# Clears off GpSimd, a later place for the decay's powers, the mixer's state recurrence on VectorE, and the last early modulation moved into the first feed-forward

## The chip, the cores and the metric

One core of a Trainium2 chip runs the whole program. The metric is the time of one execution on the device in microseconds (us); lower is better. TensorE (PE in the profile) multiplies matrices, VectorE (DVE), ScalarE (ACT) and GpSimd (POOL) work element by element, and SyncE (SP) issues nearly all transfers from the chip's memory.

## The reference

`first_block` followed by `second_block`, on 256 tokens of 1024 features in float32. Only the first block is touched by the change:

```python
mod = silu(cond) @ w_mod + b_mod                       # 9 vectors of 1024: shift, scale, gate three times
(sh1, sc1, g1, sh2, sc2, g2, sh3, sc3, g3) = split(mod, 9)
h = modulate(rms_norm(x, ffn1_norm), sh1, sc1)
x = x + 0.5 * g1 * swiglu(h, ffn1_w_gate, ffn1_w_up, ffn1_w_down)
h = modulate(rms_norm(x, mix_norm), sh2, sc2)
b_gate, c_gate, v, u = split(h @ w_in, 4)
y_conv = short_conv_mixer(b_gate, c_gate, v, conv_w)   # b_gate * conv3(c_gate * v)
y_ssm = s5_mixer(u, ...)                               # linear recurrence with complex decay, gelu, gated unit
x = x + g2 * (concat(rms_norm(y_conv), rms_norm(y_ssm)) @ w_out)
h = modulate(rms_norm(x, ffn2_norm), sh3, sc3)         # sc3 is modulation 7
x = x + 0.5 * g3 * swiglu(h, ffn2_...)
```

## The kernel before

**Precision and weights.** Every weight matrix comes in tiles of 128x2048 float32 (1 MB) through three buffers called `stage`. A tile is split into two parts: ScalarE rounds it to `wh` (line 185), VectorE takes the rest `wl = stage - wh` (line 187). A product is then three TensorE products. `Stream.schedule()` fixes the order of all tiles; `Stream.prep` loads and splits them in that order as far as four slots for split weights allow, and a transfer is issued when the tile three places ahead of it in the order has been used up.

**Modulations.** A tile of `w_mod` (a "chunk"; four chunks make one modulation) isn't split: VectorE multiplies it by the condition and adds it into `macc` with two instructions of 128x1024 (lines 853 and 855). `macc` has two buffers, and a modulation's buffer is free once TensorE has summed it over the partitions (`mod_reduce`, lines 871 and 876). Modulations 0 and 1 come first, 2 to 6 within the first feed-forward (`ffn1`), 7 within the mixer.

**The first feed-forward.** `turn` multiplies the first weights while the tokens are brought over: `evac(0)` and `evac(1)` modulate the two halves of the tokens into `hT`. Then come steps 1 to 10. A step has two products `up` (gate and up), the hidden tile (`hidf`, line 477), one product `acc` with an earlier `down` tile, and a side piece. All instructions of an engine run in the order in which the code issues them.

**The state-space set-up.** `Ssm` clears its buffers (lines 592 to 595), then computes the decay on GpSimd in `prepare`, its powers in `powers`, and from a TensorE transpose on (`s_end`, in steps 2 to 4) the `readout` and the `tables`; steps 7 to 9 make the lag kernel (`s_lag`). `powers` has one VectorE instruction, the reciprocal of line 680, between GpSimd ones.

**The mixer.** Projections `proj(ch)` alternate with the convolution (`conv_a`, `conv_v`, `conv_b`) and the recurrence (`turning(h)`, two halves, lines 1139 to 1152), whose 14 instructions are shared by VectorE (`vt`) and GpSimd (`gt`). `outputs(h)` multiplies the states, `gelu(h)` moves them on.

Of the kernel before, what the change touches and what calls it, by code (L numbers as in the profile page):

```python
# [31 lines left out]

MODS_FFN1 = (2, 3, 4, 5, 6)
MODS_MIXER = (7,)
MODS_FFN2 = (8,)
# [20 lines left out]
def schedule():  # L56
# [4 lines left out]
    def w(name, i=0):  # L61
        it.append((name, i))
# [42 lines left out]
    swap(2)  # L105
    md = [4 * g + c for g in MODS_MIXER for c in range(4)]
    for c in (6, 7, 2, 4, 0, 3, 5, 1):
        w("w_in", c)
        if c in (0, 3, 5, 1):
            w("w_mod", md.pop(0))  # L110
    w("w_out", 0)
# [96 lines left out]
class Net:  # L208
# [219 lines left out]
    def turn(self, tail, evac, chunks, use):  # L428
# [5 lines left out]
        if tail is None:  # L434
            evac(0)
            evac(1)
        else:
            for part in tail.parts[0]:
                part()
            tail.post(0)  # L440
            early = len(tail.parts[1]) - tail.late
            for part in tail.parts[1][:early]:
                part()
            S.prep(S.n_take + 1)
            evac(0)
            for part in tail.parts[1][early:]:
                part()
            S.prep(S.n_take + 2)
            tail.post(1)
            if self.after_tail is not None:  # L450
                self.after_tail()
                self.after_tail = None
            S.prep(S.n_take + n_c)
# [124 lines left out]
class Ssm:  # L578


    def __init__(self, N, p):
        self.N, self.p = N, p
        t = N.t2
        self.out = [t([16, 160], "s_out%d" % c) for c in range(2)]
        self.end = [t([16, 128], "s_end%d" % c) for c in range(2)]
        self.lag = t([16, 128], "s_lag")
        p0 = t([2, 16, 32], "s_tab2")
        self.p0 = [p0[:, c] for c in range(2)]
        self.small = t([24, 16], "s_small")
        g = N.nc.gpsimd  # L590
        self.first()
        g.memset(p0, 0.0)
        for c in range(2):
            g.memset(self.out[c], 0.0)
        g.memset(self.lag, 0.0)

# [121 lines left out]
    def step(self, s):  # L718

        N = self.N  # L720
        nc = N.nc
        if 2 <= s <= 4:
            for b in ((0, 1), (2, 3, 4), (5, 6, 7))[s - 2]:
                c, q0 = divmod(4 * b, 16)
# [4 lines left out]
                nc.scalar.copy(out=self.end[c][:, q0:q0 + 4, :], in_=pv)  # L729
            if s == 4:  # L730
                self.readout()
                self.tables()
# [64 lines left out]
def build(N):  # L797
# [117 lines left out]
    mod_reduce(1, lambda: N.bank_a("mod"))  # L915
    ssm.powers()
    xns = {}
# [31 lines left out]
    def side1(s):  # L949
# [4 lines left out]
    tail_places("ffn1_w_down", 10, 0)  # L954
    tail = N.ffn(None, lambda i: N.evac_mod(pts[i], i, modf[:, 1, :], modf[:, 0, :], N.hT),
                 ("ffn1_w_gate", "ffn1_w_up"), "ffn1_w_down", 11, True, post_ffn1, side1, 1)
    mods_ready()


    tail = mixer(N, tail, evac_mod(1), ssm, dict(  # L960
        convw=sv["conv_w"], glub=sv["glu_b"], onorm=sv["out_norms"], ones=ones, xns=xns, mods=mods_ready))

# [86 lines left out]
def mixer(N, tail, evac, ssm, c):  # L1049
    nc, t, take = N.nc, N.t, N.take  # L1050
    ones, onorm = c["ones"], c["onorm"]
    x = N.x
    vt, gt, act = nc.vector.tensor_tensor, nc.gpsimd.tensor_tensor, nc.scalar.activation
    us, cts = [], []
# [29 lines left out]

    def proj(ch):
        ps = N.bank_u("proj")
        N.feat(take("w_in", ch), N.hT, v3(ps, 2))
        N.S.free()
        return ps
# [17 lines left out]

    def conv_b(h):
        ks = slice(2 * h, 2 * h + 2)
        vt(out=flat(yc[:, ks, :]), in0=proj(h), in1=flat(conv_in[h]), op=MUL)  # L1110
        act(out=yq[:, ks, :], in_=yc[:, ks, :], func=AF.Square)
# [7 lines left out]
    conv_a(0, ps)  # L1119
    conv_v(0, vps)  # L1120

# [11 lines left out]
    def turning(h, m):  # L1133
# [6 lines left out]
        vt(out=m[1], in0=wi, in1=sin, op=MUL)  # L1140
        gt(out=m[0], in0=m[0], in1=m[1], op=ADD)
        vt(out=m[2], in0=wi, in1=cos, op=MUL)
        vt(out=m[3], in0=wr, in1=sin, op=MUL)
        gt(out=m[2], in0=m[2], in1=m[3], op=SUB)
        nc.vector.tensor_tensor_scan(out=m[1], data0=rho, data1=m[0], initial=0.0, op0=MUL, op1=ADD)
        vt(out=sr, in0=m[1], in1=cos, op=MUL)
        gt(out=si, in0=m[1], in1=sin, op=MUL)
        nc.vector.tensor_tensor_scan(out=m[3], data0=rho, data1=m[2], initial=0.0, op0=MUL, op1=ADD)
        vt(out=m[0], in0=m[3], in1=sin, op=MUL)
        gt(out=m[2], in0=m[3], in1=cos, op=MUL)  # L1150
        vt(out=sr, in0=sr, in1=m[0], op=SUB)
        gt(out=si, in0=si, in1=m[2], op=ADD)

# [25 lines left out]

    turning(0, [t([512], "hm", bufs=2), t([512], "hm", bufs=2)] + pair(t([1024], "macc", bufs=2)))  # L1180
    turning(1, [t([512], "hidh1"), t([512], "hidl1")] + pair(t([1024], "macc", bufs=2)))
    conv_b(0)
    conv_a(1, proj(3))
    outputs(0)
    gelu(0)
    conv_v(1, proj(5))
    conv_b(1)
    outputs(1)

# [11 lines left out]
    for k in range(4):  # L1201
        gain_split(yc, 0, k, hc)
    hy = (t([4, S], "hTh", F32R), t([4, S], "hTl", F32R))
    y[1] = N.t2([2, 4, 64], "s_tab0")
# [18 lines left out]
    conv_part(0, 1)  # L1223
    c["mods"]()
    ps = sums(yq)
# [683 lines left out]
```

## Time and profile before

| | |
|---|---|
| median of three runs | 1220.27 us (1218.33 to 1220.82) |
| the profiled execution | 1219.3 us |
| its span in the profile | 1217.6 us |
| granted TensorE clock, mean | 0.959 |
| busy share: TensorE, VectorE, ScalarE, GpSimd | 93%, 65%, 50%, 19% |

The span is that of one execution under the profiler; 1.7 us of its own time lie outside it. Terms below are made against 1219.3 us, and the median lies 1.0 us above that. A busy TensorE is not one at full rate, so waits are read from rows and not from its share.

### The profile page before, as it was taken

How to read it: one execution, taken by the hardware profiler on the slowest of the kernel's cores; microseconds unless marked ns; L12 is line 12 of the kernel's file. 1: busy time of each engine (PE TensorE's matmuls, PEld its weight loads, DVE VectorE, ACT ScalarE, POOL GpSimd, SP SyncE). 2: the span in 40 equal slices, each digit the busy share in tenths (PEclk: the TensorE clock that was granted, in tenths of full speed). 3: DMA queues.
4: the chain of work that ended last, by engine and by line, in shares of the span. 5: the costliest groups of instructions: out<-in, count | busy, mean ns of one | idle time of the engine just before them, and what ended most of it. 6: DMA issues, size and time to landing. Idle time of an engine off the chain costs nothing.

```text
span 1217.6 us, 18757 instructions
## 1 busy us (share of the span) xinstructions
PE 1135.3 (93%) x7780; PEld 1051.7 (86%) x7780; DVE 793.7 (65%) x934; ACT 613.4 (50%) x941; POOL 236.6 (19%) x304
## 2 busy tenths in 40 slices
PE   1698999989789999999798999999999899999998
PEld 1697999979778999998798889999989897999997
DVE  7698797667968785565466665644468776564541
ACT  3444434455084554354364656655446764664541
POOL 8996399400500000000224100000000000000000
PEclk9698999989789999999897999999999899999999
DMA  8588787535243786565043245755625332385540
GB/s 318 225 327 308 249 322 281 202 139 208 88 155 139 260 324 213 189 242 181 30 144 135 90 141 202 251 178 199 205 107 194 118 118 108 124 291 194 183 143 35
DMA packets 33093, 230.13 MB, mean 189 GB/s; under 512 B 3680, under 2 KB 4064, under 8 KB 5872
## 3 DMA queue, kind: packets, MB, share of 16 engines
q1 hardware_dynamic: 31536, 224.05, 51.2%
q10 hardware_dynamic: 1472, 4.88, 1.1%
q8 instruction: 61, 1.00, 0.3%
q14 instruction: 24, 0.20, 0.0%
HBM read 227.87 MB, written 1.05 MB: 188 GB/s over the span
## 4 chain that ended last, share of the span: by engine, by line
PE 66%; DVE 16%; ACT 8%; POOL 4%; issue 3%; DMA 2%; ACTq 0%; DVEq 0%; POOLq 0%
PE acc L262 26%; PE up L262 25%; PE turn L262 7%; DVE wl L187 7%; ACT wh L185 2%; PE kqv L262 2%; DVE macc L855 1%; POOL s_small L626 1%; PE xnT L349 1%; POOL s_small L629 1%; PE lev L1385 1%; DMA stage<-in_ffn_w_up 1%; PE glu L262 1%; ACT s_lag L748 1%; POOL E L1363 1%
## 5 line engine op out<-in xcount | busy, mean ns | idle before, releaser
L187 DVE TENSOR_TENSOR wl<-stage,wh 128x1024 fp32r<-128x1024 f32 x351 | 425.7, 1261 | 131.3 <-ACT wh L185 131.1
L185 ACT CAST wh<-stage 128x1024 fp32r<-128x1024 f32 x351 | 346.8, 1045 | 126.1 <-PE acc L262 31.4
L262 PE MATMUL up<-hTh,wh 128*128 128x256 f32 x1024 | 289.2, 282 | 1.9 <-ACT s_end L729 1.9
L262 PE MATMUL up<-hTl,wh 128*128 128x256 f32 x1024 | 287.8, 281 | 0.0
L262 PE MATMUL up<-hTh,wl 128*128 128x256 f32 x1024 | 287.8, 281 | 0.0
L262 PEld LDWEIGHTS up<-hTh,wh 128*128 128x128 f32 x1024 | 193.9, 189 | 4.4 <-ACT s_end L729 2.3
L262 PEld LDWEIGHTS up<-hTh,wl 128*128 128x128 f32 x1024 | 196.2, 192 | 0.0
L262 PEld LDWEIGHTS up<-hTl,wh 128*128 128x128 f32 x1024 | 193.6, 189 | 1.5 <-issue 0.2
L262 PE MATMUL acc<-wh,hidh 128*128 128x512 f32 x288 | 115.0, 399 | 4.0 <-ACT wh L185 3.7
L262 PE MATMUL acc<-wl,hidh 128*128 128x512 f32 x288 | 114.0, 396 | 0.8 <-DVE wl L187 0.8
L262 PE MATMUL acc<-wh,hidl 128*128 128x512 f32 x288 | 113.9, 395 | 0.3 <-DVE hidl L296 0.3
L262 PE MATMUL turn<-wh,hTh 128*128 128x256 f32 x320 | 91.4, 286 | 6.2 <-ACT hTh L290 6.2
L262 PE MATMUL turn<-wl,hTh 128*128 128x256 f32 x320 | 90.9, 284 | 2.1 <-DVE wl L187 2.1
L262 PE MATMUL acc<-wh,macc 128*128 128x512 f32 x288 | 92.7, 391 | 0.0
L262 PE MATMUL turn<-wh,hTl 128*128 128x256 f32 x320 | 91.0, 285 | 0.2 <-DVE hTl L291 0.2
L855 DVE SCALAR_TENSOR_TENSOR macc<-stage,cact,macc 128x1024 f32<-128x1024 f32 x63 | 86.1, 1367 | 3.1 <-DMA stage<-in_w_mod 1.4
L262 PEld LDWEIGHTS acc<-wh,hidh 128*128 128x128 f32 x288 | 55.1, 191 | 15.5 <-ACT wh L185 4.1
L262 PEld LDWEIGHTS turn<-wh,hTh 128*128 128x128 f32 x320 | 61.3, 192 | 6.8 <-ACT hTh L290 6.5
L262 PEld LDWEIGHTS acc<-wh,hidl 128*128 128x128 f32 x288 | 54.9, 191 | 13.3 <-DVE hidl L296 1.0
L262 PEld LDWEIGHTS acc<-wl,hidh 128*128 128x128 f32 x288 | 55.0, 191 | 12.1 <-DVE wl L187 1.8
L262 PEld LDWEIGHTS turn<-wl,hTh 128*128 128x128 f32 x320 | 61.2, 191 | 3.1 <-DVE wl L187 2.8
L262 PEld LDWEIGHTS acc<-wh,macc 128*128 128x128 f32 x288 | 54.1, 188 | 11.0
(401 smaller groups left out, 2020.0 us busy)
## 6 DMA issues: line engine op xcount, KB each, us to landing
stage<-in_w SPq DMA_DIRECT2D x64, 1024.0 KB, 4.8
stage<-in_w_mod SPq DMA_DIRECT2D x36, 1024.0 KB, 4.9
stage<-in_ffn_w_gate SPq DMA_DIRECT2D x22, 1024.0 KB, 4.8
stage<-in_ffn_w_up SPq DMA_DIRECT2D x22, 1024.0 KB, 5.0
stage<-in_ffn_w_down SPq DMA_DIRECT2D x22, 1024.0 KB, 5.2
stage<-in_a_in SPq DMA_DIRECT2D x12, 1024.0 KB, 4.9
stage<-in_w_in SPq DMA_DIRECT2D x8, 1024.0 KB, 5.0
stage<-in_w_kv SPq DMA_DIRECT2D x8, 1024.0 KB, 4.9
```

Source lines behind the costliest of these rows:

```text
L185: nc.scalar.copy(out=h[:, b:e], in_=st[:, b:e])
L187: nc.vector.tensor_tensor(out=lo[:, b:e], in0=st[:, b:e], in1=h[:, b:e].bitcast(F32), op=SUB)
L262: self.nc.tensor.matmul(out, lhs(l, k), rhs(r, k), start=first and n == 0, stop=last and n == 3 * n_k - 1)
L349: self.nc.tensor.transpose(out, src, self.ident)
L626: g.tensor_tensor(out=o, in0=x, in1=y, op=op)
L629: g.tensor_scalar(out=o, in0=x, scalar1=s1, scalar2=s2, op0=op0, op1=op1)
L748: nc.scalar.copy(out=self.lag[32 * i:32 * i + 32, 4 * b:4 * b + 4, 32 * i:128], in_=ks[:32, :, 0:128 - 32 * i])
L855: nc.vector.scalar_tensor_tensor(out=acc, in0=wv[:, k, :], scalar=cc, in1=acc, op0=MUL, op1=ADD)
L1363: gt(out=ev[:, :, 1, :], in0=bv[:, :, 1, :], in1=ref, op=SUB)
L1385: nc.tensor.matmul(ps[:, 64 * e:64 * e + 64], ks[:, 128 * e:128 * e + 128], qs[:, 64 * e:64 * e + 64], start=True, stop=True)
```

## The change

Five pieces. (1) The clears of the two `out` buffers go from GpSimd to VectorE, that of `lag` to ScalarE; they are issued first. (2) `powers` is called after the second evacuation, not ahead of the first, and the second weight is split between the two evacuations. (3) The transposes `s_end`, and what follows them on GpSimd, go from steps 2 to 4 to steps 3 to 5. (4) Modulation 7's four chunks go from the mixer into `ffn1`. (5) In the mixer all of `turning` runs on VectorE; its first half stands ahead of the first convolution, its second half behind the projections 0, 3 and 5; `gelu(0)` comes after the convolution's gain, and the last projection's `take` no longer runs ahead.

```diff
-MODS_FFN1 = (2, 3, 4, 5, 6)
-MODS_MIXER = (7,)
+MODS_FFN1 = (2, 3, 4, 5, 6, 7)
...
     for c in (6, 7, 2, 4, 0, 3, 5, 1):
         w("w_in", c)
-        if c in (0, 3, 5, 1):
-            w("w_mod", md.pop(0))
...
             evac(0)
+            S.prep(S.n_take + 2)
             evac(1)
...
-        self.first()
         g.memset(p0, 0.0)
         for c in range(2):
-            g.memset(self.out[c], 0.0)
-        g.memset(self.lag, 0.0)
+            N.nc.vector.memset(self.out[c], 0.0)
+        self.first()
+        N.nc.scalar.activation(out=self.lag, in_=N.ident.unsqueeze(1).to_broadcast([128, 16, 128]), func=AF.Copy, scale=0.0)
...
-        if 2 <= s <= 4:
-            for b in ((0, 1), (2, 3, 4), (5, 6, 7))[s - 2]:
+        if 3 <= s <= 5:
+            for b in ((0, 1), (2, 3, 4), (5, 6, 7))[s - 3]:
...
-            if s == 4:
+            if s == 5:
                 self.readout()
                 self.tables()
...
-    ssm.powers()
...
+    def evac_first(i):
+        N.evac_mod(pts[i], i, modf[:, 1, :], modf[:, 0, :], N.hT)
+        if i:
+            ssm.powers()
...
-    conv_v(0, vps)
...
-        gt(out=m[0], in0=m[0], in1=m[1], op=ADD)
+        vt(out=m[0], in0=m[0], in1=m[1], op=ADD)
...
     turning(0, [t([512], "hm", bufs=2), t([512], "hm", bufs=2)] + pair(t([1024], "macc", bufs=2)))
+    conv_v(0, vps)
+    conv_b(0, proj(0))
+    conv_a(1, proj(3))
+    vps = proj(5)
     turning(1, [t([512], "hidh1"), t([512], "hidl1")] + pair(t([1024], "macc", bufs=2)))
-    conv_b(0)
-    conv_a(1, proj(3))
     outputs(0)
-    gelu(0)
-    conv_v(1, proj(5))
-    conv_b(1)
+    conv_v(1, vps)
+    conv_b(1, proj(1, 0))
     outputs(1)
...
         gain_split(yc, 0, k, hc)
+    gelu(0)
...
-    c["mods"]()
```

Three places on VectorE, in the order in which it runs its instructions. The first is at the two evacuations (`hm`, `hTl`) ahead of the first products; before, the reciprocal stands ahead of both:

```order
L882 SCALAR_TENSOR_TENSOR modf<-modf,pack 128x8
L680 RECIPROCAL s_small<-s_small 128x16
L380 TENSOR_SCALAR hm<-xnT,modf 128x128 x4
L291 TENSOR_TENSOR hTl<-hm,hTh 128x4x128 x2
L380 TENSOR_SCALAR hm<-xnT,modf 128x128 x4
L291 TENSOR_TENSOR hTl<-hm,hTh 128x4x128 x2
L187 TENSOR_TENSOR wl<-stage,wh 128x1024 x2
```

And in the changed kernel, where the reciprocal stands behind both and the second weight's split between them:

```order
L879 SCALAR_TENSOR_TENSOR modf<-modf,pack 128x8
L376 TENSOR_SCALAR hm<-xnT,modf 128x128 x4
L287 TENSOR_TENSOR hTl<-hm,hTh 128x4x128 x2
L183 TENSOR_TENSOR wl<-stage,wh 128x1024 x2
L376 TENSOR_SCALAR hm<-xnT,modf 128x128 x4
L287 TENSOR_TENSOR hTl<-hm,hTh 128x4x128 x2
L677 RECIPROCAL s_small<-s_small 128x16
```

What moved: the reciprocal went six rows down, and `wl` two rows up.

The second place is the mixer from the copies of `u4` (`gate<-macc`) on, before. Three more chunks of modulation 7 (`macc<-stage`) and the convolution `conv_v(0)` stand ahead of the first half of the recurrence (`hm<-ssm_w`):

```order
L1079 COPY gate<-macc 32x4x64 x6
L187 TENSOR_TENSOR wl<-stage,wh 128x1024 x2
L855 SCALAR_TENSOR_TENSOR macc<-stage,cact,macc 128x1024 x2
L187 TENSOR_TENSOR wl<-stage,wh 128x1024 x2
L855 SCALAR_TENSOR_TENSOR macc<-stage,cact,macc 128x1024 x2
L1098 TENSOR_TENSOR hidh<-proj,act 128x512
```

And in the changed kernel:

```order
L1079 COPY gate<-macc 32x4x64 x6
L183 TENSOR_TENSOR wl<-stage,wh 128x1024 x4
L1138 TENSOR_TENSOR hm<-ssm_w,s_tab 128x512
L1139 TENSOR_TENSOR hm<-ssm_w,s_tab 128x512
L1140 TENSOR_TENSOR hm<-hm 128x512
L1141 TENSOR_TENSOR macc<-ssm_w,s_tab 128x512
```

What moved: the chunks are gone, the recurrence follows the splits, and its sums (line 1140) are VectorE's.

The third place is step 3 of the first feed-forward, changed kernel, between the hidden tiles (`hidf`) of steps 2 and 3:

```order
L474 TENSOR_TENSOR hidf<-up,act 128x512
L287 TENSOR_TENSOR xn<-hidf,xn 128x512
L183 TENSOR_TENSOR wl<-stage,wh 128x1024 x2
L869 TENSOR_TENSOR gate<-mod,gate 128x512 x2
L183 TENSOR_TENSOR wl<-stage,wh 128x1024 x2
L852 SCALAR_TENSOR_TENSOR macc<-stage,cact,macc 128x1024 x2
L183 TENSOR_TENSOR wl<-stage,wh 128x1024 x2
L850 TENSOR_SCALAR macc<-stage,cact 128x1024
L852 SCALAR_TENSOR_TENSOR macc<-stage,cact,macc 128x1024 x3
```

What moved: the last two rows hold two chunks where the step had one, and so it is in the steps 2 to 5 by VectorE's order.

## Rows read from the trace of the kernel before

**Rows 1.** Busy time by stretch: PE, PEld, DVE, ACT, POOL, granted clock, DMA share, GB/s

```profile
60.00:110.00 50.00, 45.17 (x298) 41.15 (x297) 47.05 (x38) 20.97 (x25) 48.56 (x40) 0.90 0.87 319
110.00:150.00 40.00, 40.00 (x308) 38.05 (x307) 28.20 (x26) 19.54 (x25) 8.94 (x10) 1.00 0.75 268
286.60:352.40 65.80, 54.56 (x423) 54.10 (x422) 57.07 (x66) 24.14 (x40) 18.96 (x18) 0.85 0.45 166
```

**Rows 2.** Timeline to the first products: start, time, engine, line, instruction, [idle before <- releaser]

```profile
5.92 4.41 POOL L594 MEMSET s_out<- 128x2560 f32 x2
6.40 6.22 DVE L853 TENSOR_SCALAR macc<-stage,cact 128x1024 f32<-128x1024 f32 x1 [6.40 <-DMA stage<-in_w_mod]
...
13.67 0.63 ACT L311 ACTIVATE hm<-x 128x512 bf16<-128x512 f32 x1 [8.41 <-DMA x<-in_x]
13.96 12.28 SPq L156 DMA_DIRECT2D stage<-in_w_mod  x5
...
24.60 9.21 DVE L855 SCALAR_TENSOR_TENSOR macc<-stage,cact,macc 128x1024 f32<-128x1024 f32 x7
...
41.45 0.25 DVE L680 RECIPROCAL s_small<-s_small 128x16 f32<-128x16 f32 x1 [3.57 <-POOL s_small L626]
...
43.59 0.58 PE L262 MATMUL turn<-wh,hTh 128*128 128x256 f32 x1 [6.16 <-ACT hTh L290]
```

**Rows 3.** TensorE's wait for a split, 44 to 250 us: total, times, longest

```profile
PE turn L262 <- DVE wl L187: 1.1, 1, 1.1
```

**Rows 4.** VectorE's groups from 60 to 110 us: count | busy, mean ns | idle before

```profile
L187 DVE TENSOR_TENSOR wl<-stage,wh 128x1024 fp32r<-128x1024 f32 x18 | 25.5, 1462 | 1.4 <-ACT wh L185 1.4
L855 DVE SCALAR_TENSOR_TENSOR macc<-stage,cact,macc 128x1024 f32<-128x1024 f32 x11 | 16.7, 1517 | 0.2
```

**Rows 5.** The split's group from 114 to 142 us

```profile
L187 DVE TENSOR_TENSOR wl<-stage,wh 128x1024 fp32r<-128x1024 f32 x8 | 9.4, 1222 | 4.5 <-ACT wh L185 4.5
```

**Rows 6.** VectorE's timeline in the first feed-forward, steps 2 to 7

```profile
98.43 0.68 DVE L477 TENSOR_TENSOR hidf<-up,act 128x512 f32<-128x512 f32 x1
...
124.33 2.36 DVE L187 TENSOR_TENSOR wl<-stage,wh 128x1024 fp32r<-128x1024 f32 x2 [3.40 <-ACT wh L185]
...
189.81 0.68 DVE L477 TENSOR_TENSOR hidf<-up,act 128x512 f32<-128x512 f32 x1
```

**Rows 7.** The chain that ended last, in order of time: start, time, what

```profile
69.97 4.82 DMA stage<-in_ffn_w_up
...
102.19 13.67 PE up L262 x96
...
122.63 10.91 PE up L262 x96
```

**Rows 8.** GpSimd's timeline at the transposes

```profile
142.21 0.40 POOL L768 TENSOR_SCALAR s_out<-s_tab 64x256 f32<-64x256 f32 x1 [19.56 <-PE s_end L349]
```

**Rows 9.** VectorE's groups in the mixer, 286 to 353 us

```profile
L855 DVE SCALAR_TENSOR_TENSOR macc<-stage,cact,macc 128x1024 f32<-128x1024 f32 x7 | 9.0, 1283 | 0.2
L1148 DVE TENSOR_TENSOR_SCAN macc<-s_tab,macc 128x512 f32<-128x512 f32 x2 | 4.6, 2281 | 0.0
...
L1142 DVE TENSOR_TENSOR macc<-ssm_w,s_tab 128x512 f32<-128x512 f32 x2 | 1.4, 686 | 0.0
...
L1145 DVE TENSOR_TENSOR_SCAN hidl<-s_tab,hidh 128x512 f32<-128x512 f32 x1 | 1.2, 1225 | 0.1
...
L853 DVE TENSOR_SCALAR macc<-stage,cact 128x1024 f32<-128x1024 f32 x1 | 0.7, 747 | 0.0
```

**Rows 10.** VectorE's timeline in the mixer

```profile
308.15 0.69 DVE L1139 TENSOR_TENSOR hm<-ssm_w,s_tab 128x512 f32<-128x512 f32 x1
...
328.46 3.42 DVE L187 TENSOR_TENSOR wl<-stage,wh 128x1024 fp32r<-128x1024 f32 x2
...
369.12 1.06 DVE L1247 TENSOR_TENSOR s_end<-xn,s_ttmp 128x256 f32<-128x256 f32 x2
```

More of the change, by code (lines that the diff above doesn't have):

```diff
@@ L105, in schedule @@
     swap(2)
-    md = [4 * g + c for g in MODS_MIXER for c in range(4)]
     for c in (6, 7, 2, 4, 0, 3, 5, 1):
         w("w_in", c)
-        if c in (0, 3, 5, 1):
-            w("w_mod", md.pop(0))
     w("w_out", 0)
@@ L954, in build @@
     tail_places("ffn1_w_down", 10, 0)
-    tail = N.ffn(None, lambda i: N.evac_mod(pts[i], i, modf[:, 1, :], modf[:, 0, :], N.hT),
-                 ("ffn1_w_gate", "ffn1_w_up"), "ffn1_w_down", 11, True, post_ffn1, side1, 1)
+    def evac_first(i):
+        N.evac_mod(pts[i], i, modf[:, 1, :], modf[:, 0, :], N.hT)
+        if i:
+            ssm.powers()
+    tail = N.ffn(None, evac_first, ("ffn1_w_gate", "ffn1_w_up"), "ffn1_w_down", 11, True, post_ffn1, side1, 1)
     mods_ready()
     tail = mixer(N, tail, evac_mod(1), ssm, dict(
-        convw=sv["conv_w"], glub=sv["glu_b"], onorm=sv["out_norms"], ones=ones, xns=xns, mods=mods_ready))
+        convw=sv["conv_w"], glub=sv["glu_b"], onorm=sv["out_norms"], ones=ones, xns=xns))
     def after_mixer():
@@ L1052, in mixer @@
     x = N.x
-    vt, gt, act = nc.vector.tensor_tensor, nc.gpsimd.tensor_tensor, nc.scalar.activation
+    vt, act = nc.vector.tensor_tensor, nc.scalar.activation
     us, cts = [], []
@@ L1083, in mixer, with proj @@
     cw = c["convw"]
-    def proj(ch):
+    def proj(ch, ahead=10 ** 9):
         ps = N.bank_u("proj")
-        N.feat(take("w_in", ch), N.hT, v3(ps, 2))
+        N.feat(take("w_in", ch, ahead), N.hT, v3(ps, 2))
         N.S.free()
@@ L1106, in conv_v, with conv_b @@
         conv_in[h] = o
-    def conv_b(h):
+    def conv_b(h, ps):
         ks = slice(2 * h, 2 * h + 2)
-        vt(out=flat(yc[:, ks, :]), in0=proj(h), in1=flat(conv_in[h]), op=MUL)
+        vt(out=flat(yc[:, ks, :]), in0=ps, in1=flat(conv_in[h]), op=MUL)
         act(out=yq[:, ks, :], in_=yc[:, ks, :], func=AF.Square)
@@ L1140, in turning @@
         vt(out=m[1], in0=wi, in1=sin, op=MUL)
-        gt(out=m[0], in0=m[0], in1=m[1], op=ADD)
+        vt(out=m[0], in0=m[0], in1=m[1], op=ADD)
         vt(out=m[2], in0=wi, in1=cos, op=MUL)
         vt(out=m[3], in0=wr, in1=sin, op=MUL)
-        gt(out=m[2], in0=m[2], in1=m[3], op=SUB)
+        vt(out=m[2], in0=m[2], in1=m[3], op=SUB)
         nc.vector.tensor_tensor_scan(out=m[1], data0=rho, data1=m[0], initial=0.0, op0=MUL, op1=ADD)
         vt(out=sr, in0=m[1], in1=cos, op=MUL)
-        gt(out=si, in0=m[1], in1=sin, op=MUL)
+        vt(out=si, in0=m[1], in1=sin, op=MUL)
         nc.vector.tensor_tensor_scan(out=m[3], data0=rho, data1=m[2], initial=0.0, op0=MUL, op1=ADD)
         vt(out=m[0], in0=m[3], in1=sin, op=MUL)
-        gt(out=m[2], in0=m[3], in1=cos, op=MUL)
+        vt(out=m[2], in0=m[3], in1=cos, op=MUL)
         vt(out=sr, in0=sr, in1=m[0], op=SUB)
-        gt(out=si, in0=si, in1=m[2], op=ADD)
+        vt(out=si, in0=si, in1=m[2], op=ADD)
     def pair(ab):
```

## The prediction

> **What bounds the kernel now.** I read the busy time by stretch first. From 60 to 110 us VectorE is busy for 47.05 of 50 us, from 110 to 150 us for 28.20 of 40 us, and in the mixer (286.6 to 352.4 us) for 57.07 of 65.8 us [rows 1]. TensorE shows as busy nearly throughout, which by itself tells little, so I went on to the chain that ended last: between 60 and 100 us it runs through VectorE's splits and through transfers such as the one of 4.82 us at 69.97 us [rows 7], and through the mixer it runs over VectorE's rows. The reader is to see that in the first feed-forward and in the mixer the stream of tiles, handled by VectorE through three buffers, sets the end, and that TensorE catches up with it wherever it waits. The later three quarters of the program are not touched; they only shift.
>
> **Part 1, the start.** The first chunk's multiplication took 6.22 us; the same instruction takes 0.747 us elsewhere [rows 2, 9]. It ran while GpSimd's clears ran (the two of `out` from 5.92 us, 4.41 us together), so 5.5 us of it is waiting. With the clears gone the chunks meet the next limit, the transfers: x, fourth in the queue behind three chunks, lands at 13.67 us, and the fourth chunk is requested only at 13.96 us, once a buffer is free [rows 2]. In the changed kernel that buffer is free some 5 us earlier, so the chunk follows x directly. At the 319 GB/s of a crowded stretch [rows 1] 1.05 MB takes 3.3 us: it lands at 17.0 us, and its two instructions (9.21/7 = 1.32 us each [rows 2]) end at 19.6 us. Before, the four chunks ended at 6.40 + 6.22 + 9.21 = 21.8 us. Gain 2.2 us; bounds 0 (transfers hold everything) and 5.5 us.
>
> The new places of the clears must be covered. No row shows VectorE clearing 2560 elements. By its rate in the one-input instruction (0.747 us for 1024) two take 3.7 us, by that of the three-operand one (1.283 us [rows 9]) 6.4 us; VectorE has nothing to do in the first 6.40 us [rows 2], and a chunk that came late by the little that the start-up takes would still wait for the fourth transfer: nothing. The Trainium skill (VectorE: DVE Perf Modes, "Zero memsets can be issued as uint32 (trn2)") has a memset take one cycle per element; at that price, an estimate of 2.7 us each, the sum is the same. No row shows a VectorE memset here. ScalarE's clear of 2048 elements, at 0.63 us per 512 [rows 2] some 2.5 us, lies in its 8.41 us of idle time before x lands.
>
> The reciprocal: VectorE stood 3.57 us at it, for GpSimd, and 0.25 us in it, with both evacuations behind it and TensorE's first product behind those (it started after 6.16 us of waiting [rows 2]). Behind the evacuations GpSimd will have finished: 3.8 us. Should it not have, `hidf` and the splits would stand behind it instead. GpSimd's powers then start behind both evacuations and a split, not ahead of them; the transposes that need them stand a step later too. Splitting the second weight between the evacuations takes away TensorE's one wait for that split, 1.1 us [rows 3]. Start in all: 2.2 + 3.8 + 1.1 = 7.1 us.
>
> **Part 2, four more chunks in the first feed-forward.** Each is one transfer on SP's queue and two VectorE instructions. The first falls into the contended stretch (2 x 1.517 = 3.0 us [rows 4]) and into a VectorE that is full, so it is paid: 3.0 us. The other three (2 x 1.283 = 2.6 us each, 7.8 us) fall into steps 3 to 5, where 40 - 28.2 = 11.8 us are idle [rows 1]. That idle time is of the kind of the 3.40 us at 124.33 us [rows 6]: ScalarE stands at a copy of the transposes or at a full slot because VectorE and ScalarE are ahead of TensorE. In the changed kernel they are behind, so they don't stand there; I let the 7.8 us vanish in the 11.8, and 1.5 of the other 4.0 us become a gain. Bounds: all 10.8 us paid, or 3.0 - 4.0 = 1.0 us gained. The transfers have room: their share in that stretch is 0.75, and four tiles of 3.3 us are 13 us over four steps.
>
> Two waits are new. The first product of modulation 5 takes the buffer of modulation 3 and so waits until TensorE has summed that, at the end of step 4; `hidf` of step 4 and all splits queue behind it. By the sum above VectorE comes there a few us after TensorE has passed, so I price it at nothing; if VectorE were on time it would stand for most of a product `acc`. And GpSimd's `readout` waits for the last transposes (142.21 us before [rows 8]) a step later. It and the tables then run against VectorE some 10 us later in the stream: less contention at their start, more at the end of the feed-forward. A split costs 1.462 us in the contended stretch and 1.222 in the quiet one [rows 4, 5]; some eight splits move against it, five out of it: 3 x 0.24, taken as 0.5 us.
>
> First feed-forward: 7.1 - 3.0 + 1.5 - 0.5 = 5.1 us earlier.
>
> **Part 3, the mixer.** VectorE loses the chunks, 0.7 + 9.0 = 9.7 us [rows 9]. It gains 12 instructions of 0.69 us, six in each half of the recurrence, but loses GpSimd beside it: a scan took 2.28 us there and 1.23 us alone [rows 9]. The two halves took 328.46 - 308.15 = 20.3 us [rows 10]; on VectorE alone, with 12 such instructions and two scans in each, they are 2 x (12 x 0.69 + 2 x 1.23) = 21.5 us end to end, a little less where they overlap. I take no change. The split behind them took 3.42 us [rows 10] where 2 x 1.222 is the quiet price: 1.0 us. With the new order the gated unit's split (2.4 us) and `gelu(0)` come behind the second convolution, which is so much earlier again; that is only postponed. And it has a price: the next feed-forward's first tile is now requested only when the gated unit's weight is split, and ScalarE, with the sigmoids behind it, waits for its 4.82 us [rows 7] while VectorE does two splits (4.9 us); the rounding of the late tile, about 1 us, is open. So 9.7 + 1.0 - 1.0 = 9.7 us by the first product of the gate (369.12 us before [rows 10]). Bounds: 4 us, if the whole 4.82 us and 1 us more show; 13.1 us, if nothing is given back and the postponed split (2.4 us) is hidden too. The sum over partitions of modulation 7 on TensorE moves to the end of the first feed-forward, where TensorE waits for splits; I count nothing.
>
> **Sum.** 1219.3 - 5.1 - 9.7 = 1204.5 us.
>
> **Rivals.**
> *The chunks are paid in full.* For it: VectorE is the bound at both ends of those steps. Then the feed-forward is 10.8 - 7.1 - 1.5 = some 2 us later or equal, and the total about 1211 us. Chance 0.18.
> *The mixer keeps its front.* If the transfer of the late tile is faster, or TensorE's products there finish under the earlier sigmoids, the mixer gains 13.1 us, and all 4.0 us of idle time show: 1219.3 - 7.6 - 13.1 = 1198.6 us, or 1195.3 us with 5.5 us at the first chunk instead of 2.2. Chance 0.12.
> *Slower: TensorE starves at a low clock.* The product `up` of step 3, right behind a wait, took 13.67 us for 96 where 10.91 is the rate of the next [rows 7]; the granted clock over that stretch was 0.90, against 1.00 in the next [rows 1]. If six tiles per step leave TensorE waiting in each of the eight steps 3 to 10, each wait costs 2.8 us more at the lower clock: 22 us, and that decides from the sixth such step on (14.8/2.8 = 5.3). Against it: split tiles stand ready in four slots, and TensorE can idle without the end moving as long as VectorE sets it. With all eight: 1227 us. Chance 0.08.
> *The lock at the end.* GpSimd's tables beside the last splits may cost a whole GpSimd instruction of about 1 us, not 0.24: eight splits, 6 us more, 1210 us; chance 0.04. The Trainium skill (SBUF — State Buffer, "Who interferes with whom") says that a two-input VectorE instruction and a GpSimd instruction that reads the memory exclude each other for a whole instruction; the means of rows 4 and 5 differ by far less.
> *The clears do nothing*, because transfers hold the first chunks: 1206.7 us, inside the likeliest case. No change at all would need two parts to cancel: 0.03.
>
> **How the numbers follow.** Likeliest (1200 to 1209 us): 0.55. Faster by over 0.2% (about what a measurement tells from no change, 2.4 us) holds that and the first two rivals and the lock: 0.89; within 0.2%: 0.03; slower: 0.08. For 8 in 10 I reach to 1194 us for the mixer's front and to 1213 us for chunks paid in full and the lock.
>
> **What would show it.** The first chunk's multiplication near 0.75 us; no idle time at the reciprocal, and TensorE's first product at about 37 to 38 us; `hidf` of step 7 (189.81 us before [rows 6]) at 184 to 185 us with no wait at modulation 5's first product; scans at 1.23 us; the gate's first product at about 354 us, with ScalarE idle for a transfer just ahead of it. The prediction is wrong if TensorE shows waits for splits with a low clock in steps 3 to 10, or if VectorE stands for TensorE in step 4.

## The result and the profile after

The changed kernel takes 1209.75 us (median of 4 runs, 1208.43 to 1210.63), the kernel before 1219.8 us on the same chip; the ratio is 0.9916, 95% interval 0.9900 to 0.9931. One execution of the kernel "start alone" below, at 2238.68 us, was in a disturbed state and is left out of its median. The forecast was 1204.5 us with 1194 to 1213 us around it: the sign and the range were right, but 10.1 us came where 14.8 were forecast, and they did not come where the sum put them. The mixer's first product starts at 270.07 us, before at 268.48: the first feed-forward ends 1.6 us **later**, where 5.1 us earlier was forecast. From there to the first product of the next feed-forward it is 109.63 us (379.70 - 270.07), before 121.81 (390.29 - 268.48): the mixer gives 12.2 us, where 9.7 were forecast. So the time lies within the range partly by luck: the first feed-forward missed by 6.7 us, and the mixer by 2.5 us the other way.

Busy time by stretch in the changed kernel (the columns are those of [rows 1]):

```profile
60.00:110.00 50.00, 47.84 (x328) 43.38 (x328) 46.62 (x38) 19.52 (x23) 48.66 (x42) 1.00 0.87 314
110.00:150.00 40.00, 31.38 (x222) 29.62 (x221) 33.12 (x30) 16.21 (x21) 9.74 (x9) 0.87 0.87 342
150.00:190.00 40.00, 40.00 (x285) 36.96 (x284) 35.63 (x32) 15.46 (x19) 29.38 (x26) 1.00 0.80 296
```

From 110 to 150 us VectorE was idle 11.8 us before and is idle 6.9 us now: the added chunks filled 4.9 us, not all. TensorE, which was busy there throughout, now stands idle for 8.6 us, at a granted clock of 0.87, and the transfers' share rose from 0.75 to 0.87. The timeline of VectorE, from the start to step 9 (to be held against [rows 2, 6]):

```profile
1.41 2.19 DVE L590 MEMSET s_out<- 128x2560 f32 x1 [1.41 <-PEq L1901]
4.08 2.19 DVE L590 MEMSET s_out<- 128x2560 f32 x1 [0.48 <-issue]
7.22 0.75 DVE L850 TENSOR_SCALAR macc<-stage,cact 128x1024 f32<-128x1024 f32 x1 [0.95 <-DMA stage<-in_w_mod]
...
45.30 0.25 DVE L677 RECIPROCAL s_small<-s_small 128x16 f32<-128x16 f32 x1
...
131.55 0.75 DVE L850 TENSOR_SCALAR macc<-stage,cact 128x1024 f32<-128x1024 f32 x1 [0.49 <-DMA stage<-in_w_mod]
...
146.58 2.36 DVE L183 TENSOR_TENSOR wl<-stage,wh 128x1024 fp32r<-128x1024 f32 x2 [2.50 <-ACT wh L181]
...
190.54 0.68 DVE L474 TENSOR_TENSOR hidf<-up,act 128x512 f32<-128x512 f32 x1
...
227.15 3.68 DVE L183 TENSOR_TENSOR wl<-stage,wh 128x1024 fp32r<-128x1024 f32 x2 [3.06 <-ACT wh L181]
230.75 4.27 DVE L852 SCALAR_TENSOR_TENSOR macc<-stage,cact,macc 128x1024 f32<-128x1024 f32 x2
234.94 4.29 DVE L183 TENSOR_TENSOR wl<-stage,wh 128x1024 fp32r<-128x1024 f32 x2
```

The start went as forecast: the first chunk takes 0.75 us, the reciprocal has no idle time ahead of it, and `hidf` of step 2 comes 3.3 us earlier (95.10 us). By step 7 nothing is left: 190.54 us, before 189.81 [rows 6]. The first product of modulation 5 (131.55 us) waits 0.49 us for its transfer and not for TensorE. At 227 to 239 us pairs of splits and products that take 2.4 to 2.6 us alone take 3.7 to 4.3 us. GpSimd fills its tables then, in its timeline:

```profile
226.70 1.05 POOL L597 TENSOR_TENSOR s_tab<-s_tab,s_small 128x512 f32<-128x512 f32 x1
227.71 2.03 POOL L598 TENSOR_TENSOR s_ttmp<-s_tab,s_small 128x512 f32<-128x512 f32 x1
229.82 2.12 POOL L599 TENSOR_TENSOR s_tab<-s_tab,s_ttmp 128x512 f32<-128x512 f32 x1
```

The product that began before VectorE's split took 1.05 us, those beside its splits and products 2.0 to 2.1 us. TensorE's timeline has a wait that the prediction did not have, in step 4 (two more for `hidf`, of 2.2 and 1.5 us, stand at 95.83 and 115.31 us):

```profile
38.31 0.58 PE L258 MATMUL turn<-wh,hTh 128*128 128x256 f32 x1 [2.57 <-ACT hTh L286]
...
134.37 1.09 PE L345 MATMUL s_end<-ident,s_out 128*128 128x128 f32 x4 [5.26 <-DVE hidf L474]
137.31 0.58 PE L258 MATMUL up<-hTh,wh 128*128 128x256 f32 x1 [1.85 <-ACT s_end L726]
```

The chain that ended last, in order of time, shows what follows:

```profile
125.14 6.32 DMA stage<-in_w_mod
...
137.31 13.66 PE up L258 x96
...
159.47 11.38 PE up L258 x96
...
178.04 11.31 PE up L258 x96
```

The transposes of step 4 take PSUM banks (TensorE's result memory) from the four that `up` uses; one is free only when `hidf` of step 4 has read it, 5.26 us late. That `hidf` (133.54 us) stands behind the two products of a chunk whose transfer, 6.32 us long, starts the piece of the chain shown first: it is requested at 125.14 us, when VectorE has used up a buffer. After the stand the 96 products of `up` take 13.66 us, the next ones 11.38. From 137.31 to 196.7 us the chain is TensorE's alone. In the kernel before it is so from 102.19 us [rows 7] on, up to 195.6 us; three more pieces of its chain:

```profile
142.04 10.90 PE up L262 x96
...
158.40 11.31 PE up L262 x96
...
176.82 11.41 PE up L262 x96
```

So from step 3 to step 7 TensorE set the pace before, and a step that is late there is not made up. The mixer, on VectorE (to be held against [rows 9, 10]):

```profile
303.13 1.22 DVE L1144 TENSOR_TENSOR_SCAN hm<-s_tab,hm 128x512 f32<-128x512 f32 x1
...
312.36 2.35 DVE L183 TENSOR_TENSOR wl<-stage,wh 128x1024 fp32r<-128x1024 f32 x2
...
346.47 6.90 DVE L183 TENSOR_TENSOR wl<-stage,wh 128x1024 fp32r<-128x1024 f32 x6 [0.26 <-ACT wh L181]
354.71 2.36 DVE L183 TENSOR_TENSOR wl<-stage,wh 128x1024 fp32r<-128x1024 f32 x2 [1.34 <-ACT wh L181]
...
359.02 1.14 DVE L1247 TENSOR_TENSOR s_end<-xn,s_ttmp 128x256 f32<-128x256 f32 x2 [1.62 <-ACT xn L1245]
```

Scans and split have their quiet prices, the gate's first product is 10.1 us earlier, and it stands behind the late tile, as forecast.

### The profile page after: what moved, and what is told of

Same layout as the page of the kernel before. It is cut to its first block, busy times and chain, and to the rows that moved or that the text cites. A ratio compares the mean times of both kernels' runs of the same rounds, so it can differ in the third digit from the quotient of the medians.

```text
span 1207.6 us, 18756 instructions
## 1 busy us (share of the span) xinstructions
PE 1132.4 (94%) x7780; PEld 1048.9 (87%) x7780; DVE 791.8 (66%) x946; ACT 615.2 (51%) x942; POOL 214.5 (18%) x291
## 3 DMA queue, kind: packets, MB, share of 16 engines
HBM read 227.87 MB, written 1.05 MB: 190 GB/s over the span
## 4 chain that ended last, share of the span: by engine, by line
PE 65%; DVE 18%; ACT 8%; DMA 4%; issue 3%; POOL 1%; ACTq 0%; SPq 0%; DVEq 0%
PE up L258 24%; PE acc L258 24%; PE turn L258 8%; DVE wl L183 8%; PE kqv L258 3%; ACT wh L181 3%; DVE macc L852 2%; DMA stage<-in_w_mod 2%; PE vg L258 2%; PE lev L1385 1%; PE xnT L345 1%; DMA stage<-in_ffn_w_gate 1%; DMA stage<-in_ffn_w_up 1%; DVE x L395 1%; DVE act L394 1%
```

## The experiments

The theory after the result: the four extra chunks are paid for almost in full, and it is the steps they fall into that make them dear. Rivals: the start's gain would have been lost in the stream anyway; the transposes' new place costs it; GpSimd's tables at the end take it. The results together are in the table below (times in us; `hidf` of steps 7 and 9, first product of the mixer and of the next feed-forward from the profiled execution of each). The kernel before ran again beside each group of kernels, with medians from 1218.23 to 1220.79 us, so two rows are best compared by their ratios. Two profiles of the same code up to the mixer, the changed kernel's and that of GpSimd in the recurrence, differ by 5.9 us at `hidf` of step 9 and by 2.0 us at the mixer's start, so smaller differences there say little.

| kernel | median | ratio to before (95%) | hidf 7 | hidf 9 | mixer | next |
|---|---|---|---|---|---|---|
| before | 1219.8 | | 189.81 | 236.99 | 268.48 | 390.29 |
| changed | 1209.75 | 0.9916 (0.9900 to 0.9931) | 190.54 | 239.16 | 270.07 | 379.70 |
| start alone | 1219.94 | 1.0000 (0.9983 to 1.0018) | 187.80 | 235.19 | 267.04 | 389.06 |
| start and step | 1212.93 | 0.9947 (0.9933 to 0.9962) | 180.18 | 229.98 | 261.64 | 383.40 |
| chunks in the mixer | 1214.35 | 0.9960 (0.9945 to 0.9975) | 180.33 | 229.92 | 260.63 | 383.93 |
| small products | 1204.99 | 0.9893 (0.9869 to 0.9917) | 185.31 | 233.78 | 264.80 | 374.75 |
| no transfer | 1210.04 | 0.9928 (0.9912 to 0.9944) | 188.43 | 236.80 | 268.89 | 378.63 |
| no tables | 1202.31 | 0.9860 (0.9844 to 0.9877) | 190.72 | 232.11 | 262.40 | 372.28 |
| GpSimd in the recurrence | 1210.87 | 0.9927 (0.9909 to 0.9945) | 189.63 | 233.30 | 268.06 | 380.26 |
| extras in steps 7 to 10 | 1205.85 | 0.9900 (0.9877 to 0.9923) | 183.39 | 235.38 | 265.27 | 375.34 |
| extras in steps 5 to 8 | 1208.15 | 0.9914 (0.9884 to 0.9944) | 189.94 | 235.89 | 267.04 | 376.93 |
| extras in 4, 6, 8, 10 | 1207.79 | 0.9899 (0.9877 to 0.9922) | 186.36 | 236.58 | 266.53 | 376.54 |
| two late, two in the tail | 1204.38 | 0.9871 (0.9849 to 0.9893) | 182.84 | 233.46 | 264.59 | 374.75 |
| and late tile behind | 1204.91 | 0.9872 (0.9846 to 0.9898) | 183.32 | 234.42 | 265.75 | 377.47 |

**Small products.**

```diff
+            m = 8 if 4 * g + c in (14, 17, 20, 23) and (c or k) else D
-                ...(out=acc, in0=wv[:, k, :], scalar=cc, in1=acc, ...)
+                ...(out=acc[:, :m], in0=wv[:, k, :m], scalar=cc, in1=acc[:, :m], ...)
```

> The changed kernel, but the four extra chunks of the first feed-forward (14, 17, 20 and 23, one in each of steps 3 to 6) are still transferred and multiplied on 8 of their 1024 columns only (the first product of chunk 20, which starts a sum, stays whole); the result of modulations 3 to 5 is so incomplete. If VectorE's products are what the extra chunks cost, hidf of step 7 comes at 184 to 185 us instead of 190.5 and the kernel takes 1203 to 1205 us. If their transfers are the cost, nothing moves by more than 1 us: 1209 to 1210 us. If TensorE's own waits for PSUM banks in step 4 (5.3 us) come from the new place of the transposes and not from VectorE being late, again 1209 to 1210 us, and the 5.3 us wait stays.

1204.99 us, `hidf` of step 7 at 185.31 us, the mixer 5.3 us earlier than in the changed kernel (3.3 us against the second profile of its code): VectorE's products are that much of the price by the profiles; the intervals of the ratios overlap. But the stand in step 4 stays (4.9 us), and 185.3 is not the 180.2 of kernels with no extra chunk at all: a chunk that is only transferred still costs something.

**No transfer.**

```diff
+        upto += sum(n == "w_mod" and j in (14, 17, 20, 23) for n, j in self.items[self.n_prep:upto])
...
+            if name == "w_mod" and j in (14, 17, 20, 23):
+                self.staged[i] = None
+                self.n_load += 1
+                continue
...
-        wv = v3(st, 2)
+        wv = x if st is None else v3(st, 2)
```

> The changed kernel, but the same four extra chunks are not transferred: VectorE multiplies x in their place (two whole products each, so modulations 3 to 5 are wrong), and the next tile is requested instead. If the transfers of 3.1 us each are the cost, hidf of step 7 comes 5 us or more earlier than 190.5 us and the kernel takes 1203 to 1205 us. If VectorE's products are the cost, the time stays within 2 us of 1209.7 us.

No change in time, 1210.04 us; 1.2 us at the mixer's start are within what two profiles differ. The transfer alone is not the price. Products gone, 5.3 us come back; transfers gone, 1 us; both gone, 9.4 us ("chunks in the mixer", 270.07 - 260.63). Against the second profile each is 2.0 us less, and both gone still give more than the two together (7.4 us): where either is left, it holds part of what the other would give back.

**Start alone.** The kernel before with the edits to `Ssm.__init__`, `turn` and `evac_first` of the change, and nothing else.

> The kernel before with the start alone: clears off GpSimd, powers behind the second evacuation, the second weight's split between the evacuations. Nothing else. If the extra chunks are what used up the start's gain, the 7 us arrive at the end of the first feed-forward and the kernel takes 1212 to 1214 us. If the stream (transfers, splits) would have taken the gain back in any case, it takes 1217 to 1219 us.

No gain at all: 1219.94 us. TensorE reaches its first product as early as in the changed kernel, and stands in step 2 for GpSimd, whose powers now start later. TensorE's timeline:

```profile
99.20 1.97 PE L349 MATMUL s_end<-ident,s_out 128*128 128x128 f32 x8 [12.95 <-POOL s_out L713]
```

The kernel before, TensorE's waits from 44 to 250 us:

```profile
PE s_end L349 <- POOL s_out L712: 2.4, 1, 2.4
```

The rival held as to the time, though not by its reason: the stream took nothing back, one wait did.

**Start and step.** The same with the transposes moved:

```diff
-        if 2 <= s <= 4:
+        if 3 <= s <= 5:
```

> The kernel before with the start's edits and, beside them, the transposes of steps 2 to 4 moved to steps 3 to 5; chunks and mixer as before. The start's edits alone gave nothing, since TensorE stood 13.0 us in step 2 for GpSimd's powers. If that wait was all that took the start's gain, the first feed-forward now ends 6 to 7 us earlier than before and the kernel takes 1212 to 1214 us. If VectorE's stream takes it back anyway, 1217 us or more.

1212.93 us, 0.9947; `hidf` of step 7 is 9.6 us earlier than before and the mixer starts 6.8 us earlier. So the start is worth its 7 us, but only together with the later transposes. The transposes' move without the start was not run; what it could take away in the kernel before is the wait of 2.4 us. 2.6 us of the 9.6 go between steps 7 and 9, where GpSimd's tables now lie; that is less than two profiles of the same code differ there.

**Chunks in the mixer.** The changed kernel with

```diff
-MODS_FFN1 = (2, 3, 4, 5, 6, 7)
+MODS_FFN1 = (2, 3, 4, 5, 6)
+MODS_MIXER = (7,)
```

and the loop over w_in tiles and the sum's call as before.

> The changed kernel with modulation 7's four chunks back in the mixer, where they stood before (one behind each of four w_in tiles, the sum behind the first products of the mixer's end); start, step of the transposes and the mixer's new order stay. If the chunks alone used up the start's gain, the first feed-forward ends some 7 us earlier than before (mixer's first product at 261 to 262 us) and the mixer, with the chunks paid at 9.7 us, gains 2 to 3 us: 1209 to 1211 us in all, about the same as the changed kernel. If the new place of the transposes holds TensorE in step 4 even without the chunks, the mixer starts at 266 us or later: 1213 to 1216 us.

1214.35 us. The first theory was right on the first feed-forward (mixer at 260.63 us), and wrong on the mixer: from its first product to that of the next feed-forward it takes 123.30 us, 1.5 us longer than before, so the chunks cost 123.30 - 109.63 = 13.7 us there and not 9.7. Six other kernels with the changed mixer take 109.74 to 110.07 us for it, so this difference is far outside the scatter. VectorE's timeline shows the rest:

```profile
281.09 0.75 DVE L854 TENSOR_SCALAR macc<-stage,cact 128x1024 f32<-128x1024 f32 x1
281.87 1.28 DVE L856 SCALAR_TENSOR_TENSOR macc<-stage,cact,macc 128x1024 f32<-128x1024 f32 x1
...
289.75 2.60 DVE L856 SCALAR_TENSOR_TENSOR macc<-stage,cact,macc 128x1024 f32<-128x1024 f32 x2
...
350.46 0.17 DVE L881 TENSOR_TENSOR modf<-mod,pack 128x8 f32<-128x8 f32 x1 [3.79 <-PE mod L877]
```

Beside the products VectorE stands 3.79 us for TensorE's sum of modulation 7, with three pairs of splits and the gate behind it; the kernel before has the same wait:

```profile
361.94 0.17 DVE L880 TENSOR_TENSOR modf<-mod,pack 128x8 f32<-128x8 f32 x1 [4.01 <-PE mod L876]
```

**No tables.** The cosine and sine tables are filled by two clears instead of the loop of products, which is taken out whole (the states are then wrong):

```diff
-        g.memset(self.cos[:, :, 0:1], 1.0)
-        g.memset(self.sin[:, :, 0:1], 0.0)
+        g.memset(self.cos, 1.0)
+        g.memset(self.sin, 0.0)
...
```

> The changed kernel without the products that fill the cosine and sine tables on GpSimd (they are filled with a constant by two clears, so the mixer's states are wrong). If GpSimd beside VectorE makes the last splits and products dear (pairs of 2.4 to 2.6 us took 3.7 to 4.3 us at 227 to 239 us), hidf of step 9 comes 4 to 5 us earlier than 239.2 us and the kernel takes 1204 to 1206 us. If that contention is the 0.5 us of the prediction, or TensorE sets the pace there, 1209 us.

1202.31 us, a larger gain than expected. Up to step 7 nothing differs (190.72 us); from step 7 to step 9 it takes 41.39 us, in the changed kernel 48.62 and in the second profile of its code 43.67. At the mixer's start the difference is 7.7 and 5.7 us, and by the ratios of the medians 6.8: the tables cost some 6 to 8 us of the first feed-forward. The instructions that took 3.68, 4.27 and 4.29 us above:

```profile
225.04 2.36 DVE L183 TENSOR_TENSOR wl<-stage,wh 128x1024 fp32r<-128x1024 f32 x2 [3.06 <-ACT wh L181]
227.32 2.60 DVE L841 SCALAR_TENSOR_TENSOR macc<-stage,cact,macc 128x1024 f32<-128x1024 f32 x2
229.84 2.35 DVE L183 TENSOR_TENSOR wl<-stage,wh 128x1024 fp32r<-128x1024 f32 x2
```

The cost is not new: the kernel before takes 47.18 us from step 7 to step 9, "start and step" 49.80. What the change added to it can't be told, since the two profiles of the changed code lie 5.0 us apart (48.62 and 43.67), depending on which of VectorE's instructions meet the tables.

**GpSimd in the recurrence.** Six instructions of each half back on GpSimd:

```diff
-        vt(out=m[0], in0=m[0], in1=m[1], op=ADD)
+        gt(out=m[0], in0=m[0], in1=m[1], op=ADD)
...
-        vt(out=si, in0=si, in1=m[2], op=ADD)
+        gt(out=si, in0=si, in1=m[2], op=ADD)
```

> The changed kernel with the six instructions of each half of the recurrence back on GpSimd, in the new order of the mixer. If VectorE alone takes as long as the two engines together, as predicted, the time stays within 1 us of 1209.7 us. If what GpSimd slows on VectorE beside it (scans of 2.28 instead of 1.22 us, the split behind the halves) is worth more, now that no chunk stands between, it is 2 to 4 us slower: 1212 to 1214 us.

1210.87 us, 1.1 us more, with intervals that overlap. On VectorE the first half goes from 297.47 to 307.78 us, 10.3 us, in the changed kernel from 299.28 to 309.26, 10.0 us. The forecast of no change holds for the halves. But the mixer as a whole takes 112.20 us (380.26 - 268.06), against 109.63 to 110.07 us in the seven kernels with the recurrence on VectorE, so the move is worth 2.1 to 2.6 us by the profile; the halves show 0.6 of it, and where the rest lies was not followed up.

**Where the extras fall.** Three kernels change only the condition that places them in the list of tiles:

```diff
-            if s > 2 and len(md) > 2 * (10 - s):
+            if s > 6 and len(md) > 2 * (10 - s):
```

(`s > 4` for steps 5 to 8; every even step from 4 on for the third.)

> The changed kernel with the four extra chunks in steps 7 to 10 instead of 3 to 6. If the price of a chunk is set by how full VectorE and the transfers are where it falls (VectorE 27.5 of 40 us busy and the transfers' share 0.63 from 190 to 230 us), the first feed-forward ends 4 to 5 us earlier: 1204 to 1206 us. If GpSimd's tables beside the last steps make each product dear there, or the last steps have to wait for the late chunks, 1210 to 1214 us.

> The changed kernel with the extra chunks in steps 5 to 8. In the changed kernel TensorE stood 5.3 + 1.8 us in step 4 and ran the next 96 products at 13.7 instead of 11.4 us, some 9 us together, about what the chunks cost; with no extra chunk ahead of step 5 that stand is gone. If it is the way in which the chunks are paid, the mixer starts at 263 to 266 us and the kernel takes 1203 to 1206 us, no slower than with steps 7 to 10. If a chunk costs its products wherever VectorE is full (35.6 of 40 us from 150 to 190 us, beside GpSimd), the mixer starts at 267 to 270 us: 1207 to 1210 us.

> The changed kernel with one extra chunk in each of steps 4, 6, 8 and 10. If a step has some slack of its own which takes one chunk and is made up again in the next, the mixer starts at 263 to 265 us and the kernel takes 1203 to 1205 us. If each chunk pushes the steps behind it by its products and nothing is made up, it is like the changed kernel: 268 to 270 us, 1208 to 1210 us.

1205.85, 1208.15 and 1207.79 us. Against the 260.63 us of no extra chunk the mixer starts 4.6, 6.4 and 5.9 us later, in the changed kernel 9.4 (7.4 in the second profile). As times none of the three differs from the changed kernel: the intervals overlap. With steps 7 to 10 and 5 to 8 the stand of 5.3 us in step 4 is gone (TensorE stands 3.2 us for GpSimd at the first transposes instead, and with steps 5 to 8 also 3.1 us for `hidf`), and in the latter most of the price stays: the stand is not how the chunks are paid for, only where it shows. With extras in 7 to 10 they run into the tables instead; TensorE's wait there:

```profile
232.34 0.58 PE L258 MATMUL up<-hTh,wh 128*128 128x256 f32 x1 [9.28 <-ACT act L473]
```

**Two late, two in the tail.** Extras in steps 8 and 10, and the last two chunks behind the last splits of the first feed-forward and behind the mixer's fourth tile; the sum behind the first half of the recurrence:

```diff
     for c in (6, 7, 2, 4, 0, 3, 5, 1):
         w("w_in", c)
+        if c == 7:
+            w("w_mod", 30)
+        if c == 4:
+            w("w_mod", 31)
...
+    c["mods"]()
     conv_v(0, vps)
```

> The changed kernel with one extra chunk in each of steps 8 and 10 and the last two chunks of modulation 7 behind the first feed-forward: one behind the last tile split ahead of its end, one behind the mixer's fourth tile, where VectorE stood 1.5 and 3.5 us; its sum over partitions behind the first products with the states. If chunks are free where VectorE stands for TensorE (about 15 us of idle time from 247 to 282 us, no GpSimd work beside it), the kernel takes 1201 to 1204 us, less than with steps 7 to 10 (1205.9 us). If the chunk ahead of the feed-forward's end delays its norms by its 2.6 us and the other the states by as much, 1206 to 1208 us.

1204.38 us, the lowest median of the complete kernels; its interval (0.9849 to 0.9893) lies below that of the changed kernel (0.9900 to 0.9931) and still overlaps that of steps 7 to 10. VectorE's timeline shows the two moved chunks:

```profile
250.71 2.60 DVE L857 SCALAR_TENSOR_TENSOR macc<-stage,cact,macc 128x1024 f32<-128x1024 f32 x2
253.22 0.69 DVE L399 SCALAR_TENSOR_TENSOR act<-acc,gate 128x512 f32<-128x512 f32 x1
...
279.24 2.60 DVE L857 SCALAR_TENSOR_TENSOR macc<-stage,cact,macc 128x1024 f32<-128x1024 f32 x2
282.77 2.36 DVE L188 TENSOR_TENSOR wl<-stage,wh 128x1024 fp32r<-128x1024 f32 x2 [0.94 <-ACT wh L186]
```

Against the kernel with no extra chunk, `hidf` of step 10 is 3.6 us later (243.84 against 240.21 us), the mixer's start 4.0 us (264.59 against 260.63): the two in steps 8 and 10 cost 3.6, the one behind the last splits 0.3. The one behind the fourth tile costs at most 0.5 (the mixer takes 110.16 us, against 109.63 to 110.07 without). Both are within what two profiles differ: chunks where VectorE stands for TensorE are nearly free, as far as these profiles can tell.

**And late tile behind.** In that kernel ScalarE waits 2.5 us for the next feed-forward's first tile, and TensorE 4.0 us behind ScalarE; its waits from 338 to 366 us:

```profile
PE glu L263 <- ACT rs_sq L304: 4.0, 1, 4.0
PE glu L263 <- ACT wh L186: 1.9, 1, 1.9
PE glu L263 <- DVE wl L188: 0.8, 1, 0.8
```

One edit puts that tile behind both halves of the gate:

```diff
-    gw = take("glu_w")
+    gw = take("glu_w", 0, 0)
...
         if h == 0:
+            St.prep(St.n_take + 2)
```

> The kernel with two late extras and two chunks in the tail, and beside it one edit at the mixer's end: the gated unit's weight is taken alone, its second half's weights (w_out 2 and 3) are split behind the first two sigmoids, and the next feed-forward's first tile behind both halves. If ScalarE's wait for that late tile (2.5 us, and 2.0 us in its rounding, with the square root and the sigmoids queued behind) is what holds TensorE 4.0 us there, that wait goes, the next feed-forward's first product comes 3 to 5 us earlier than 374.8 us and the kernel takes 1199.5 to 1202 us. If VectorE sets the end of the mixer in any order, since it does the same splits and products, it comes within 1 us of 374.8 us: 1203.5 to 1205 us.

1204.91 us, with single runs from 1199.54 to 1208.98: as a time inconclusive. The profile is clear: the 4.0 us are gone, and two others, 2.2 and 1.7 us, stand in their place. TensorE's waits from 338 to 366 us:

```profile
PE ss L1203 <- ACT s_end L1256: 2.2, 1, 2.2
PE glu L263 <- ACT wh L186: 1.9, 1, 1.9
PE acc L263 <- DVE act L399: 1.7, 1, 1.7
PE glu L263 <- DVE wl L188: 0.8, 1, 0.8
```

The mixer takes 111.7 us, not less than 110.2. The rival's time came about. Its reason, that VectorE sets the mixer's end in any order, was not tested by itself.

## Why the prediction was right in sign and some 5 us short

*Start, 7.1 us.* Right. The four first chunks end at 19.6 us as worked out, TensorE's first product is 5.3 us earlier, its first 96 products end at 52.45 us, 7.0 earlier (59.42 before, with the wait of 1.1 us in it), and "start and step" carries 6.8 us to the mixer. The prediction costed the later transposes as a wait of GpSimd alone; their worth is that without them TensorE stands 13.0 us.

*"I let the 7.8 vanish in the 11.8, and 1.5 of the other 4.0 us become a gain."* This is the step that failed. The chunks cost 9.4 us in all (8.4 against "start and step", 7.4 by the second profile of the changed code), near the bound of 10.8 and far from the 1.5 (3.0 - 1.5) of the sum. VectorE's busy time from 110 to 150 us rose by 4.9 us, not by 7.8, and 6.9 us of idle time stayed. The reason given was that ScalarE stood only because the two were ahead of TensorE. But in the changed kernel VectorE still stands 2.50 us for ScalarE's copy at 146.58 us, which TensorE released, and ScalarE 4.42 us at 125.09 us for a tile requested only at 120.35 us. Tiles, products and `hidf` pass VectorE in one order through three buffers, so idle time in front of one of them is not room for another behind it. That is what small products and no transfer, each with a part of the price, bear out. Nor does TensorE "catch up with it wherever it waits": from 102.19 to 195.6 us the chain of the kernel before is TensorE's own, so a stand that VectorE causes there stays. That the three buffers and not another limit join the two was not tried: a fourth buffer was not built. The prediction's signs of being wrong missed this: from 44 to 250 us TensorE has no wait for a split, and modulation 5's first product does not wait for TensorE; what TensorE waits for is `hidf`.

*The rival "the chunks are paid in full"* is the one that came about for this part: "some 2 us later or equal" against the measured 1.6 us (0.4 us earlier in the second profile); its total of 1211 us lacked the mixer's surplus. *The low clock* was real in one step (13.66 instead of 11.38 us), behind the stand in step 4, and did not decide: the kernel before has such a step too (13.67 us at 102.19 us [rows 7]).

*Contention, 0.5 us.* (By its own numbers, 3 x 0.24, it is 0.7 us.) As a sum it is not settled: from `hidf` of step 7 to the mixer's first product the kernel before takes 78.67 us, the changed code 79.53 and 78.43 us in its two profiles, "start and step" 81.46. What failed is the price of 0.24 us for a split. The Trainium skill (SBUF — State Buffer, "Who interferes with whom") has a VectorE instruction with two inputs from that memory and a GpSimd instruction that reads it exclude each other for a whole instruction; the prediction held against it that the means of [rows 4, 5] differ by 0.24 us only. The rows after agree with the rule where GpSimd's instructions are long: at 227 to 239 us they are products of 128x512, 1.05 us when alone, and a pair of splits takes 4.29 instead of 2.35 us, 0.97 more for each, which is the price of the rival *the lock at the end*. From 60 to 110 us they are copies of 64x256 and products of 128x256, 0.40 and 0.62 us when alone (69.02 and 75.74 us), and a split takes 1.44 us on average, 0.26 more than alone. Beside the smallest ones, products of 128x16 that take 0.22 us alone, a split costs next to nothing more, while they take 1.2 us; VectorE and GpSimd in the changed kernel:

```profile
205.55 2.40 DVE L183 TENSOR_TENSOR wl<-stage,wh 128x1024 fp32r<-128x1024 f32 x2
```

```profile
205.68 1.19 POOL L600 TENSOR_TENSOR s_small<-s_small 128x16 f32<-128x16 f32 x1
206.84 1.20 POOL L601 TENSOR_TENSOR s_small<-s_small 128x16 f32<-128x16 f32 x1
```

The price taken from the one stretch did not hold for the other.

*Mixer, 9.7 us.* Right in mechanism, mis-sized in two terms that were counted as nothing. The chunks took 13.7 us out, not 9.7; the wait for modulation 7's sum (4.01 us), which went with them, is as long as the difference, though no run took it away alone. The prediction said "I count nothing" of the sum. The new order costs 1.5 us instead of 0 in a mixer that has the chunks ("chunks in the mixer", 123.30 against 121.81). 13.7 - 1.5 = 12.2. The scans (1.22 us), the split (2.35), the halves (20.0 us against 20.3) and the late tile came as worked out. That the late tile is what costs there was not borne out: without that wait nothing is gained. (The lower bound of 4 us counts the rounding of that tile twice: 9.7 + 1.0 - 4.8 - 1.0 is 4.9 us.)

## What to carry to other kernels

Idle time of an engine in a stretch is room for added work only where nothing that the next engine waits for stands behind the added work in the same queue: read where in the order the gap lies (a wait just ahead of the result that is late is no room), and put the work into gaps behind it. Put work that can go anywhere where its engine waits for the bound itself and GpSimd does not run beside it: here the tail, at some 0.5 us a chunk or less instead of about 2. When work is moved out of a stage, count the waits that its result causes there, not only its instructions; and when one engine is made earlier, look what it meets next.

## What the runs showed of the hardware

What GpSimd costs VectorE grows with the length of GpSimd's instruction: a split of 1024 columns takes 1.18 us alone, 1.20 us beside products of 128x16 (0.22 us alone), 1.44 us on average from 60 to 110 us beside copies and products of 0.40 to 0.62 us, and 2.14 us beside products of 128x512, which themselves go from 1.05 to 2.03 us; removing those and the shorter table products gave some 6 to 8 us back. VectorE cleared 2560 columns in 2.19 us, about two thirds of what the rate of its three-operand product (1.28 us for 1024) would give, and less than the prediction's estimate of 2.7 us: the measurement decides. After stands of 5.26 and 1.85 us TensorE ran 96 products in 13.66 us, and the next in 11.38 us; the granted clock was 0.87 from 110 to 150 us and 1.00 from 150 to 190 us.
